# A transformer encoder block in fp32: where the last query and key turns of a head pair stand, which banks the turns use, and which engine squares the tokens

## The chip, the cores and the metric

The kernel runs on one core of a Trainium2 chip. The metric is the device time of one execution in microseconds. TensorE is PE in the profile, VectorE DVE, ScalarE ACT, GpSimd POOL, and SP issues most of the DMAs.

## What is computed

One encoder layer over 1024 tokens of width 1024. Half of the mixing width is neighbourhood attention with 8 heads of 64 on a token grid, the other half a multi-scale mean pooling; then an output projection and a gated feed-forward layer.

```python
for l in range(DEPTH):
    h = rms_norm(x, norm1_g[l])
    proj = h @ w_in[l]                       # q, k, v, u
    q = rms_norm(q, q_norm_g[l])             # per head
    k = rms_norm(k, k_norm_g[l])
    a = neighbourhood_attention(q, k, v, rpb[l])
    p = multiscale_pool(u, w_pool[l], pool_scale[l])
    x = x + jnp.concatenate([a, p], axis=-1) @ w_out[l]
    h2 = rms_norm(x, norm2_g[l])
    x = x + (jax.nn.silu(h2 @ w_gate[l]) * (h2 @ w_up[l])) @ w_down[l]
```

## The kernel before

Every fp32 product is made of three passes on operands that are split into a high part (a rounded cast, on ScalarE as a rule) and a low part (source minus high part, on VectorE): high by high, high by low, low by high (`mm3`, `split`). The names end in h and l: `xh`, `xl` for the tokens, `w1h`, `w1l` for projection weights, `kh`, `kl`, `qh`, `ql`, `vnh`, `vnl` for keys, queries and values, `wuh`, `wul` for the weights of u.

**Head.** Token chunks `xh[k]`, `xl[k]` (8 of them) and the weights of pair 0 are loaded, cast and split. The 8 token tiles of pair 0 stand in 8 PSUM banks (`pj_0_0` to `pj_0_7`); the first six are accumulated together, chunk by chunk, and the last two behind them. Meanwhile each token tile `xt` is squared and summed into `ssx`, from which `rstd` comes by `rsqrt` (lines 96 to 101). `pair(tt)` takes two tiles: squares of queries and keys and their sums, the values (`proj_vals`, L283 and L285), the norms (`proj_norm`, L270). `turn(tt)` (`proj_evac_b`) transposes the normalized queries and keys of two tiles on TensorE into a bank `qkt` (L91) and splits them into `qh`, `ql` (L311, L313) and `kh`, `kl` (L112, L113). Then `u_pool` projects u (bank `pu`), scales it, and pools it.

**Pairs 1 to 3.** `g_proj(p)` is a generator that yields after each three matmuls. It projects tile by tile (`pj_p_t`, 24 matmuls of 384 columns), the first two tiles `together`, and evacuates each with `finish`: a copy `qn` (L260), values, squares, norms, and behind each second tile the turn of the two tiles before. The last turn of a pair, that of tiles 6 and 7, is left in `late`. For the last pair tiles 5, 6 and 7 are projected together, with casts of output weights `wo` and of mixed inputs `mx` in between (`first_wo`).

**Attention** runs beside it, in 16 steps (4 pairs by 4 column blocks). `step(v)` writes scores of block v into four banks `s`, the values of block v - 2 into `po`, and the transposed probabilities of block v - 1 into three banks `pt`; between these parts `more(u)` draws units from the generators by the tables `FIRST`, `CYC` and, once the projections are done, `WCYC`, which draws the output products `pw`. `flush()` runs the turn in `late`: it is called ahead of each step with v % 4 == 3, and once more within `together`.

**Banks.** PSUM has three pools: `mmp` (3 banks: `pj`, `pu`, most `pw`), `stp` (4: scores, probabilities, and turns), `pop` (1: values). Work that takes a bank waits until the last readers of the tile that had it before are done.

**Order.** While `pin` is set, TensorE's instructions stay in program order, and likewise ScalarE's and VectorE's under `pin_act` and `pin_dve`; the others are placed by the compiler's scheduler. Each engine runs its own list in order. SP's DMAs wait for the tile that they write to be free and for the lane of an earlier DMA.

## Time and profile before

| what | us |
|---|---|
| three runs | 1038.33, 1038.53, 1041.15 (median 1038.53) |
| profiled execution | 1039.33 |
| its span | 1037.5 |
| TensorE busy | 1011.6 |
| VectorE busy | 656.4 |
| ScalarE busy | 416.3 |
| GpSimd busy | 392.4 |

The span runs from the first to the last instruction on the chip; about 1.8 us of the execution lie around it. In a timeline each row has the start, the duration, engine, line, operation, output and inputs, and in brackets how long the engine had been idle before and what ended that. The duration of a matmul is longer than the distance to the next one, as matmuls are pipelined; costs of matmuls are taken from distances. Rows with windows give the length of the window, the busy time (and number of instructions) of each engine, the TensorE clock that was granted (1.00 is full), the share of the DMA engines, and GB/s.

### The profile page before, as it was taken

What the parts mean: (1) busy time and instruction counts of PE and PEld (TensorE: products, weight loads), DVE (VectorE), ACT (ScalarE), POOL (GpSimd) and SP (SyncE); (2) the same over time, 40 slices, a digit from 0 to 9 for tenths busy, and PEclk for the clock granted to TensorE, in tenths of its full rate; (3) what the DMA queues carried; (4) which work ended last, traced back from release to release, by engine and by line L of the source; (5) the groups of instructions that cost most, each with busy time, mean ns of one, the idle gap of its engine ahead of it and who ended that gap; (6) DMA issues with size and microseconds to landing.
All of it is one profiled execution on the core that took longest, in us unless ns stands there. A gap on an engine that the chain in (4) does not pass through costs nothing.

```text
span 1037.5 us, 13512 instructions
## 1 busy us (share of the span) xinstructions
PE 1011.6 (98%) x4905; PEld 861.6 (83%) x4905; DVE 656.4 (63%) x1083; ACT 416.3 (40%) x820; POOL 392.4 (38%) x428
## 2 busy tenths in 40 slices
PE   9899989999799999999999999999999999999998
PEld 9788889899688887888888888888888888888887
DVE  5577766545754568866655545555462499978872
ACT  6532656545663235523332332332331254533400
POOL 0000433232361026466667568459545310000170
PEclk9999989989899999999999999999999999999999
DMA  9411633243721223113233133133126984373302
GB/s 359 164 36 41 198 86 93 61 143 132 254 72 61 107 108 115 57 62 125 98 115 137 63 120 134 71 122 112 72 81 198 340 274 155 118 244 110 134 31 91
DMA packets 52994, 132.22 MB, mean 127 GB/s; under 512 B 5632, under 2 KB 14592, under 8 KB 52928
## 3 DMA queue, kind: packets, MB, share of 16 engines
q1 hardware_dynamic: 46000, 106.97, 30.9%
q0 software_dynamic: 5632, 20.19, 5.3%
q10 hardware_dynamic: 1296, 4.20, 1.0%
q8 instruction: 38, 0.62, 0.2%
q14 instruction: 28, 0.23, 0.1%
HBM read 96.48 MB, written 30.67 MB: 123 GB/s over the span
## 4 chain that ended last, share of the span: by engine, by line
PE 91%; DMA 3%; DVE 3%; ACT 2%; issue 1%; SPq 1%; ACTq 0%; DVEq 0%
PE x L86 12%; PE w L86 12%; PE z L86 12%; PE pw L86 8%; PE pj L86 8%; PE y L86 6%; PE pc L86 6%; PE pa L86 6%; PE pd L86 6%; PE pu L86 4%; PE po L86 3%; PE pb L86 3%; PE s L86 2%; PE pt L91 1%; DMA raw_w<-in_w 1%; DMA raw_xt<-in_xt 1%
## 5 line engine op out<-in xcount | busy, mean ns | idle before, releaser
L86 PE MATMUL x<-b_h,w 128*128 128x512 f32 x352 | 115.6, 391 | 0.0
L86 PE MATMUL pw<-wo,mx 128*128 128x512 f32 x384 | 91.4, 393 | 0.2 <-ACT mx L725 0.2
L86 PE MATMUL pj<-w1h,xh 128*128 128x384 f32 x256 | 87.7, 347 | 0.0
L86 PE MATMUL pj<-w1l,xh 128*128 128x384 f32 x256 | 85.1, 337 | 0.0
L86 PE MATMUL pj<-w1h,xl 128*128 128x384 f32 x256 | 84.0, 337 | 0.0
L86 PEld LDWEIGHTS pw<-wo,mx 128*128 128x128 f32 x384 | 70.9, 188 | 14.8 <-ACT mx L725 0.6
L592 POOL TENSOR_SCALAR e<-e,r 64x128 f32<-64x128 f32 (+2 forms) x96 | 51.8, 555 | 80.6 <-DVE r L587 63.2
L1305 POOL TENSOR_TENSOR x2r<-x2r,u 128x512 f32<-128x512 f32 x12 | 23.8, 2025 | 149.8 <-DVE u L1263 149.8
L86 PEld LDWEIGHTS x<-b_h,w 128*128 128x128 f32 x352 | 65.9, 188 | 13.7
L86 PE MATMUL x<-b_l,w 128*128 128x512 f32 x176 | 68.7, 390 | 0.0
L1024 POOL TENSOR_TENSOR ur<-ur,gr 128x512 f32<-128x512 f32 x33 | 52.6, 1595 | 40.7 <-issue 22.0
L113 DVE TENSOR_TENSOR w_s<-sa,w_s 128x512 fp32r<-128x512 f32 x44 | 48.1, 1093 | 29.4 <-ACT w_s L112 29.2
L112 ACT CAST a_h<-raw_a 128x1024 fp32r<-128x1024 f32 (+1 forms) x42 | 41.0, 978 | 49.3 <-PE pc L86 13.8
L86 PE MATMUL z<-bt_h,w_s 128*128 128x512 f32 x176 | 57.8, 389 | 0.0
L86 PE MATMUL w<-bt_h,w_s 128*128 128x512 f32 x176 | 57.8, 389 | 0.0
L86 PE MATMUL y<-bt_h,w_s 128*128 128x512 f32 x176 | 57.8, 389 | 0.0
L86 PE MATMUL w<-b_h,w_s 128*128 128x512 f32 x176 | 57.8, 389 | 0.0
L86 PE MATMUL z<-bt_h,w 128*128 128x512 f32 x176 | 57.8, 389 | 0.0
L113 DVE TENSOR_TENSOR a_l<-raw_a,a_h 128x1024 fp32r<-128x1024 f32 (+1 forms) x42 | 49.7, 1188 | 3.4 <-DMA raw_d<-in_wd 2.9
L86 PEld LDWEIGHTS pj<-w1h,xh 128*128 128x128 f32 x256 | 48.8, 191 | 0.7 <-issue 0.5
L86 PEld LDWEIGHTS pj<-w1l,xh 128*128 128x128 f32 x256 | 48.4, 189 | 0.0
L86 PEld LDWEIGHTS pj<-w1h,xl 128*128 128x128 f32 x256 | 48.3, 189 | 0.0
(257 smaller groups left out, 2680.8 us busy)
## 6 DMA issues: line engine op xcount, KB each, us to landing
raw_a<-gsd SPq DMA_DIRECT2D x77, 256.0 KB, 3.6
raw_g<-in_wgu SPq DMA_DIRECT2D x22, 512.0 KB, 3.8
raw_u<-in_wgu SPq DMA_DIRECT2D x22, 512.0 KB, 4.0
gsd<-gr POOLq DMA_DIRECT2D x22, 512.0 KB, 4.0
raw_d<-in_wd SPq DMA_DIRECT2D x20, 512.0 KB, 4.1
nb<-in_rpbx SPq DMA_DIRECT2D x24, 384.0 KB, 3.7
raw_w<-in_w SPq DMA_DIRECT2D x15, 384.0 KB, 4.1
gsd<-ur POOLq DMA_DIRECT2D x11, 512.0 KB, 3.3
```

The lines of the kernel that those rows point to most:

```text
L86: i = nc.tensor.matmul(*a, **k)
L91: i = nc.tensor.transpose(*a)
L112: keep(nc.scalar.copy(h, src))
L113: keepd(nc.vector.tensor_tensor(out=l, in0=src, in1=h.bitcast(F32), op=ALU.subtract))
L592: nc.gpsimd.tensor_scalar(out=out, in0=in0, scalar1=s1, scalar2=1.0, op0=ALU.mult, op1=ALU.mult)
L1024: eng.tensor_tensor(out=res[i][c][:, l], in0=src, in1=g, op=ALU.mult)
L1305: nc.gpsimd.tensor_tensor(out=q, in0=q, in1=U2[c], op=ALU.add)
```

## The change

- The last turn of a pair moves within the step: it was ahead of the scores of v = 3, 7, 11 and is now between the other units and the probabilities of that step. It keeps a bank of `stp`; the three other turns of a pair take a bank of `mmp`.
- The squares of token tiles 1, 3, 5 and 7 are made by VectorE (a multiply with a sum along the row, new L491), those of 0, 2, 4 and 6 by ScalarE as before.
- In the head both last tiles of pair 0 are projected right behind the first six; statistics are split into `stats_a`, `stats_b` and `stats_c`, and the first chain of norms stands ahead of the casts of `wu` and `wp`. Turns 1 to 3 and the fourth `pair` are called from `u_pool`.
- For the last pair tiles 6 and 7 are projected together, and tile 5 by itself. `WCYC` has other numbers.

```diff
--- before.py
+++ after.py
@@ -31,13 +31,12 @@
 RQ = [[0, 1], [0, 1, 2], [1, 2, 3], [2, 3]]
 KE = 2
 W0 = 42
-KSS = 6
 WARM = 17
 CYC = [3, 3, 3, 4, 4, 4, 4, 4, 4, 4, 4, 5, 5, 5, 4, 4]
 R0 = 22
 FIRST = [3, 3, 4, 4, 4, 4, 4, 4, 4, 4, 4]
 CYC3 = CYC
-WCYC = [1] + [2] * 10 + [3]
+WCYC = [1, 4, 4, 1, 1] + [2] * 6 + [3]
 POOL_W = [2, 4, 8, 16]
 DGROUPS = [3, 4, 4]
 NPF = NFC // 2
@@ -224,20 +223,26 @@
 
     y8s = {}
 
-    def proj_stats(p, tt, pss, mid=None):
-        v8 = tq.tile([P, 8], F32, name=f"v8_{p}_{tt}", tag="v8")
-        y8 = tq.tile([P, 8], F32, name=f"y8_{p}_{tt}", tag="y8")
-        y8s[p, tt] = y8
-        for i, ps in enumerate(pss):
+    v8s = {}
+
+    def stats_a(p, tt, srcs):
+        v8s[p, tt] = []
+        for i, src in enumerate(srcs):
             t = 2 * tt + i
             sq = tq.tile([P, 256], F32, name=f"sq_{p}_{t}", tag="sq", bufs=2)
-            keep(nc.scalar.activation(sq, ps[:, :256], AF.Square))
+            keep(nc.scalar.activation(sq, src[:, :256], AF.Square))
             s4 = tq.tile([P, 4], F32, name=f"s4_{p}_{t}", tag="s4")
             keepd(
                 nc.vector.tensor_reduce(
                     out=s4, in_=sq.rearrange("p (h d) -> p h d", d=HD), axis=AX.X, op=ALU.add
                 )
             )
+            v8s[p, tt].append(s4)
+
+    def stats_b(p, tt):
+        v8 = tq.tile([P, 8], F32, name=f"v8_{p}_{tt}", tag="v8")
+        for i, s4 in enumerate(v8s[p, tt]):
+            t = 2 * tt + i
             keepd(
                 nc.vector.tensor_scalar(
                     out=v8[:, 4 * i : 4 * i + 4],
@@ -248,9 +253,12 @@
                     op1=ALU.add,
                 )
             )
-        if mid:
-            mid(p, 2 * tt, pss)
-        rsqrt(tq, y8, v8, 8, f"q{p}_{tt}")
+        v8s[p, tt] = v8
+
+    def stats_c(p, tt):
+        y8 = tq.tile([P, 8], F32, name=f"y8_{p}_{tt}", tag="y8")
+        y8s[p, tt] = y8
+        rsqrt(tq, y8, v8s.pop((p, tt)), 8, f"q{p}_{tt}")
 
     def new_qn(p, t):
         return tq.tile([P, 256], F32, name=f"qn_{p}_{t}", tag="qn", bufs=5)
@@ -293,10 +301,12 @@
             )
 
     def proj_evac_a(p, tt, pss):
-        proj_stats(p, tt, pss)
+        stats_a(p, tt, pss)
+        stats_b(p, tt)
+        stats_c(p, tt)
         proj_norm(p, tt, pss)
 
-    def proj_evac_b(p, tt, pool=stp):
+    def proj_evac_b(p, tt, pool=mmp):
         (kh, kl), (qh, ql) = kT[p], qT[p]
         qk = qks.pop((p, tt))
         pt = bank(pool, f"qkt_{p}_{tt}")
@@ -370,8 +380,8 @@
                 for i in range(2):
                     R = 2 * half + i
                     nc.vector.tensor_tensor(out=uv[:, R], in0=pv[:, i], in1=rv[:, R], op=ALU.mult)
-                if g == half == 0:
-                    hook()
+                if 2 * g + half < 3:
+                    hook(2 * g + half + 1)
 
         def u_win(g):
             u = us[g]
@@ -476,11 +486,16 @@
     ssx = cp.tile([P, NT], F32, name="ssx")
     for t in range(NT):
         raw = raws.pop(("xt", t))
-        keep(nc.scalar.activation(raw, raw, AF.Square, accum_out=ssx[:, t : t + 1]))
+        acc = ssx[:, t : t + 1]
+        if t % 2:
+            nc.vector.tensor_tensor_reduce(
+                out=raw, in0=raw, in1=raw, scale=1.0, scalar=0.0, op0=ALU.mult, op1=ALU.add, accum_out=acc
+            )
+        else:
+            keep(nc.scalar.activation(raw, raw, AF.Square, accum_out=acc))
     pin_act = False
     fetch_wu(1)
     proj_alloc(0)
-    cook_wu(0)
     pj = [bank(pl, f"pj_0_{t}") for t, pl in enumerate((mmp, mmp, mmp, stp, stp, pop, stp, stp))]
     pin = True
     for k in range(KC):
@@ -489,42 +504,47 @@
             for t in ts:
                 for i in h:
                     proj_pass(0, t, pj[t], k, i)
-        if k == KSS:
-            nc.vector.tensor_scalar(
-                out=vx, in0=ssx, scalar1=1.0 / DM, scalar2=EPS, op0=ALU.mult, op1=ALU.add
-            )
-            nc.vector.tensor_scalar(out=evx, in0=vx, scalar1=EPS, scalar2=None, op0=ALU.mult)
-            rsqrt(tq, rstd, vx, NT, "x")
-            nc.vector.scalar_tensor_tensor(
-                out=qscale, in0=gqk[:, 0:1], scalar=-(HD**-0.5), in1=gqk[:, 1:2], op0=ALU.mult, op1=ALU.mult
-            )
+    for t in (6, 7):
+        for k in range(KE, KC):
+            proj_mm(0, t, pj[t], k)
     pin_act = pin_dve = True
+    stats_a(0, 0, pj[:2])
+    keepd(nc.vector.tensor_scalar(out=vx, in0=ssx, scalar1=1.0 / DM, scalar2=EPS, op0=ALU.mult, op1=ALU.add))
+    keepd(nc.vector.tensor_scalar(out=evx, in0=vx, scalar1=EPS, scalar2=None, op0=ALU.mult))
+    stats_b(0, 0)
+    rsqrt(tq, rstd, vx, NT, "x")
+    stats_c(0, 0)
+    proj_norm(0, 0, pj[:2])
+    cook_wu(0)
+    keepd(
+        nc.vector.scalar_tensor_tensor(
+            out=qscale, in0=gqk[:, 0:1], scalar=-(HD**-0.5), in1=gqk[:, 1:2], op0=ALU.mult, op1=ALU.mult
+        )
+    )
+    proj_vals(0, 0, pj[:2])
 
     def pair(tt):
         pss = pj[2 * tt : 2 * tt + 2]
-        proj_stats(0, tt, pss, proj_vals)
+        stats_a(0, tt, pss)
+        stats_b(0, tt)
+        proj_vals(0, 2 * tt, pss)
+        stats_c(0, tt)
         proj_norm(0, tt, pss)
 
-    def turn(tt):
-        proj_evac_b(0, tt, (mmp, mmp, pop, stp)[tt])
-
-    pair(0)
+    proj_evac_b(0, 0)
     pair(1)
-    for k in range(KE, KC):
-        proj_mm(0, 6, pj[6], k)
-    turn(0)
     pair(2)
-    for k in range(KE, KC):
-        if k == 5:
-            turn(1)
-        proj_mm(0, 7, pj[7], k)
-    turn(2)
-    pair(3)
     pin = pin_act = pin_dve = False
     wp_hl = slot(F32R, "wp_hl", [P, 2, 4, P])
     wps += [wp_hl[:, 0], wp_hl[:, 1]]
     cook(("wp",), *wps)
-    u_win = u_pool(up, lambda: turn(3))
+
+    def hook(tt):
+        proj_evac_b(0, tt)
+        if tt == 1:
+            pair(3)
+
+    u_win = u_pool(up, hook)
 
     def attn_alloc(p):
         mf = slot(F32, f"mixf_{p}")
@@ -644,6 +664,8 @@
             values(*blocks[v - 2])
         more(4 * v)
         more(4 * v + 1)
+        if v % 4 == 3:
+            flush()
         if 0 < v <= len(blocks):
             transposes(*blocks[v - 1])
         more(4 * v + 2)
@@ -653,7 +675,7 @@
 
     def flush():
         while late:
-            proj_evac_b(late.pop(), 3)
+            proj_evac_b(late.pop(), 3, stp)
 
     def g_proj(p):
         proj_alloc(p)
@@ -679,7 +701,7 @@
                 finish(t, ps)
 
         yield from together((0, 1), lambda kk: flush() if kk == 2 else None)
-        for t in range(2, NT - 3 * last):
+        for t in range(2, NT - 2 * last):
             ps = bank(mmp, f"pj_{p}_{t}")
             for k in range(KC):
                 proj_mm(p, t, ps, k)
@@ -696,7 +718,7 @@
                 if t == 6:
                     cook_w1(p + 1, 0)
         if last:
-            yield from together((5, 6, 7), first_wo)
+            yield from together((6, 7), first_wo)
         late.append(p)
         if p + 1 < NPAIR:
             for i in range(1, 4):
@@ -860,8 +882,6 @@
             run(WCYC[min(u - W0 - 1, len(WCYC) - 1)])
 
     for v in range(len(blocks) + 1):
-        if v % 4 == 3:
-            flush()
         step(v, more)
     run(1000)
     values(*blocks[-1])
```

VectorE, head. In the kernel before these rows follow each other (`xl_197`, `xl_205` and `xl_209` are chunks 5, 6 and 7; `w1l_3` the weights of the last two chunks):

```order
L173 SCALAR_TENSOR_TENSOR xl_193<-raw_x_130,sm_sb,xh_192 128x1024
L173 SCALAR_TENSOR_TENSOR xl_197<-raw_x_132,sm_sb,xh_196 128x1024
L113 TENSOR_TENSOR w1l_3_201<-raw_w_0_3_134,w1h_3_200 128x768
L173 SCALAR_TENSOR_TENSOR xl_205<-raw_x_136,sm_sb,xh_204 128x1024
L173 SCALAR_TENSOR_TENSOR xl_209<-raw_x_138,sm_sb,xh_208 128x1024
```

In the changed kernel, from the same row on (`raw_xt_142` and `raw_xt_146` are token tiles 1 and 3, and L491 is the square, with its sum in a second row):

```order
L172 SCALAR_TENSOR_TENSOR xl_193<-raw_x_130,sm_sb,xh_192 128x1024
L491 ISA raw_xt_142,ssx<-raw_xt_142 128x1024
L491 ISA ssx 128x1
L172 SCALAR_TENSOR_TENSOR xl_197<-raw_x_132,sm_sb,xh_196 128x1024
L112 TENSOR_TENSOR w1l_3_201<-raw_w_0_3_134,w1h_3_200 128x768
L491 ISA raw_xt_146,ssx<-raw_xt_146 128x1024
L491 ISA ssx 128x1
L172 SCALAR_TENSOR_TENSOR xl_205<-raw_x_136,sm_sb,xh_204 128x1024
L172 SCALAR_TENSOR_TENSOR xl_209<-raw_x_138,sm_sb,xh_208 128x1024
```

Two squares now stand among the splits: that of tile 1 ahead of chunk 5, that of tile 3 ahead of chunk 6.

TensorE, step 3, as pair 2 is projected beside pair 0's attention. Before, the scores follow the turn (`qkt_3_1634` is the last turn of pair 1, of whose four transposes the last two are shown; `s_3` are the scores of pair 0's block 3; the three rows ahead of the turn are those of the next piece):

```order
L91 MATMUL qkt_3_1634<-ident,qn_6_1508 128x128
L91 MATMUL qkt_3_1634<-ident,qn_7_1560 128x128
L86 MATMUL s_3_0_0_1643<-kh_225,qh_223 128x384
L86 MATMUL s_3_0_1_1644<-kh_225,qh_223 128x384
L86 MATMUL s_3_0_0_1643<-kl_226,qh_223 128x384
L86 MATMUL s_3_0_1_1644<-kl_226,qh_223 128x384
```

In the changed kernel the projection rows are followed at once by the scores:

```order
L85 MATMUL pj_1_1624<-w1h_0_1512,xh_162 128x384
L85 MATMUL pj_1_1624<-w1l_0_1513,xh_162 128x384
L85 MATMUL pj_1_1624<-w1h_0_1512,xl_163 128x384
L85 MATMUL s_3_0_0_1634<-kh_225,qh_223 128x384
L85 MATMUL s_3_0_1_1635<-kh_225,qh_223 128x384
L85 MATMUL s_3_0_0_1634<-kl_226,qh_223 128x384
```

and the turn (`qkt_3_1717`, its last two transposes) comes later in the step, behind 18 more projections and right ahead of the probabilities `pt_2`:

```order
L90 MATMUL qkt_3_1717<-ident,qn_6_1508 128x128
L90 MATMUL qkt_3_1717<-ident,qn_7_1560 128x128
L90 MATMUL pt_2_0_1726<-ident,e_2_0_0_1449 128x128 x3
L90 MATMUL pt_2_0_1726<-ident,e_2_1_0_1462 128x128
L90 MATMUL pt_2_2_1728<-ident,e_2_1_0_1462 128x128
L90 MATMUL pt_2_1_1727<-ident,e_2_0_1_1453 128x128 x3
```

The scores, the values and 18 projections have passed ahead of the turn.

VectorE, last pair. Before, the norms of tiles 4 to 7, `kl` of turn 2 and `ql` of turn 3 stand in this order, ahead of the score reductions (L574) of block 3:

```order
L270 TENSOR_TENSOR qn_4_2795<-qn_4_2795,y_3_2_3024 128x256
L270 TENSOR_TENSOR qn_5_3019<-qn_5_3019,y_3_2_3024 128x256
L99 TENSOR_TENSOR rsq_q_3_3072<-y_3_3_3061 128x8
L100 SCALAR_TENSOR_TENSOR rsq_q_3_3072<-rsq_q_3_3072,v_3_3_3060 128x8
L101 SCALAR_TENSOR_TENSOR y_3_3_3061<-rsq_q_3_3072,y_3_3_3061 128x8
L270 TENSOR_TENSOR qn_6_3052<-qn_6_3052,y_3_3_3061 128x256
L270 TENSOR_TENSOR qn_7_3056<-qn_7_3056,y_3_3_3061 128x256
L313 SCALAR_TENSOR_TENSOR ql_2338<-qkt_2_3080,qscale,qh_2337 128x4x64
L113 TENSOR_TENSOR wo_1_1_3455<-raw_wo_1_3177,wo_1_0_3454 128x512 x2
L113 TENSOR_TENSOR kl_2340<-qkt_2_3080,kh_2339 128x256
L313 SCALAR_TENSOR_TENSOR ql_2338<-qkt_3_3103,qscale,qh_2337 128x4x64
L574 ISA e_3_0_0_3130,m_3_0_0_3131<-s_3_0_0_3112,nb_3_0_2908 128x384
```

In the changed kernel `kl` of turn 2 (the last row) stands behind the score reductions of block 3 (L594, pair 2):

```order
L594 ISA e_3_1_0_3134,m_3_1_0_3135<-s_3_1_0_3105,nb_3_1_2934 128x384
L594 ISA m_3_1_0_3135 128x1
L594 ISA e_3_1_1_3138,m_3_1_1_3139<-s_3_1_1_3106,nb_3_1_2934 128x384
L594 ISA m_3_1_1_3139 128x1
L323 SCALAR_TENSOR_TENSOR ql_2338<-qkt_2_3080,qscale,qh_2337 128x4x64
L750 TENSOR_TENSOR mx_0_1_3029<-mixf_1798,mx_0_0_3028 128x512
L750 TENSOR_TENSOR mx_0_1_3029<-mixf_1136,mx_0_0_3028 128x512
L247 TENSOR_SCALAR v_3_3_3068<-s_3_7_3066,evx 128x4
L607 RECIPROCAL r_3_0_3120<-sm_3_0_3119 128x2
L112 TENSOR_TENSOR wo_0_1_3047<-raw_wo_0_2989,wo_0_0_3046 128x512 x2
L607 RECIPROCAL r_3_1_3133<-sm_3_1_3132 128x2
L112 TENSOR_TENSOR kl_2340<-qkt_2_3080,kh_2339 128x256
```

Turn 2's queries and keys are now split behind reductions, splits of mixed inputs and of output weights; turn 3 comes later still.

## The prediction

> **What bounds the kernel now.** I read the page first, then TensorE's row in the view of waits.
>
> ```profile
> PE 1011.6 (98%) x4905; PEld 861.6 (83%) x4905; DVE 656.4 (63%) x1083; ACT 416.3 (40%) x820; POOL 392.4 (38%) x428
> ```
> ```profile
> PE qkt L91 <- DVE qn L270: 10.3, 3, 5.4
> PE qkt L91 <- ACT vnh L283: 3.1, 1, 3.1
> PE s L86 <- DVE kl L113: 2.6, 3, 1.4
> PE s L86 <- DVE m L574: 1.8, 3, 0.7
> ```
>
> TensorE is busy 98% of the span and no other engine over 63%, so the end moves only where TensorE stops waiting or runs faster. The change touches four groups of waits: columns are the total, the number and the longest, 17.8 us together. The windows then show what a wait costs behind itself (second-last but two columns: granted clock).
>
> ```profile
> 40.30:43.80 3.50, 3.50 (x12) 2.86 (x11) 2.95 (x11) 1.79 (x7) 0.00 (x0) 0.51 0.02 5
> ```
> ```profile
> 149.00:153.00 4.00, 4.00 (x15) 3.56 (x16) 1.89 (x9) 2.55 (x8) 1.25 (x3) 0.50 0.50 139
> ```
> ```profile
> 210.00:214.00 4.00, 4.00 (x16) 3.61 (x14) 1.34 (x6) 2.15 (x9) 1.28 (x4) 0.50 0.62 171
> ```
> ```profile
> 266.00:270.00 4.00, 2.36 (x10) 1.38 (x10) 3.55 (x15) 1.91 (x6) 0.00 (x0) 0.50 1.04 333
> ```
>
> Behind each wait for `qkt` the clock is halved, for about 3.5 us or more. Behind the 1.38 us wait for `kl`, at 119.91, it stays whole:
>
> ```profile
> 119.90:123.30 3.40, 3.39 (x20) 3.16 (x21) 3.40 (x13) 2.65 (x8) 1.03 (x2) 1.00 0.45 126
> ```
>
> So a wait of 2.4 to 5.4 us is paid twice, once idle and once slow.
>
> **Last turn of pairs 1 and 2.** Here TensorE's timeline shows the whole stage.
>
> ```profile
> 141.55 0.42 PE L86 MATMUL pj<-w1h,xh 128*128 128x384 f32 x1
> ...
> 145.73 1.10 PE L91 MATMUL qkt<-ident,qn 128*128 128x128 f32 x4 [2.35 <-DVE qn L270]
> ...
> 148.85 0.69 PE L86 MATMUL s<-kh,qh 64*128 64x384 f32 x1 [0.45 <-DVE m L574]
> ...
> 153.27 0.34 PE L86 MATMUL pj<-w1h,xh 128*128 128x384 f32 x1
> ...
> 156.40 0.82 PE L91 MATMUL pt<-ident,e 128*128 128x128 f32 x6
> ```
> ```profile
> 250.55 0.44 PE L86 MATMUL s<-kh,qh 64*128 64x384 f32 x2
> ...
> 251.80 0.38 PE L86 MATMUL po<-pt_h,vnh 128*128 128x256 f32 x1
> ...
> 253.66 0.34 PE L86 MATMUL pj<-w1h,xh 128*128 128x384 f32 x1
> ```
> ```profile
> 201.55 0.60 PE L91 MATMUL qkt<-ident,qn 128*128 128x128 f32 x4
> 201.90 0.42 PE L86 MATMUL pj<-w1h,xh 128*128 128x384 f32 x1
> ```
>
> From 141.55 to the probabilities at 156.40 go 14.85 us. The work in it at full clock: 27 projection matmuls (9 ahead, 18 behind; the last 18 take 156.40 - 153.27 = 3.13, so 0.174 each, 4.69 in all), four transposes 0.35 (201.55 to 201.90), one score block 1.25 and one value block 1.86 (from 250.55 on): 8.15 us. So 6.7 us are idle or slow. The change puts the same pieces in the order: 9 projections, scores, values, 18 projections, turn, probabilities. The turn is then asked for 4.69 + 3.11 = 7.8 us after 141.55, at 149.35 or later.
>
> ```profile
> 142.70 0.35 DVE L285 SCALAR_TENSOR_TENSOR vnl<-pj,rstd,vnh 128x128 fp32r<-128x128 f32 x1
> ...
> 145.16 0.76 DVE L270 TENSOR_TENSOR qn<-qn,y 128x256 f32<-128x256 f32 x2
> ```
>
> Its `qn` was ready at 145.92; the score reductions now come ahead of it on VectorE, four at 0.48 (below), so about 147.9: 1.5 us early, no wait. New is a wait of projections: two mmp banks are left for tiles while `qkt` holds the third, so pair 2's tile 1 needs `vnl` of pair 1's tile 7, done at 143.05, and TensorE is there after 6 matmuls, at 142.59: 0.46. The moved turn issues four transposes, two copies on ScalarE, two subtractions on VectorE and no DMA; the next score block, its reader, comes a whole step later than it. Saved: 6.7 - 0.5 = **6.2 us**.
>
> ```profile
> 206.27 0.85 PE L91 MATMUL qkt<-ident,qn 128*128 128x128 f32 x4 [2.56 <-DVE qn L270]
> ...
> 217.21 1.04 PE L91 MATMUL pt<-ident,e 128*128 128x128 f32 x8
> ```
> ```profile
> 203.25 0.35 DVE L285 SCALAR_TENSOR_TENSOR vnl<-pj,rstd,vnh 128x128 fp32r<-128x128 f32 x1
> ```
>
> Pair 2 is the same code: 217.21 - 201.90 = 15.31 less 8.15 is 7.2; the new wait ends at 203.60, TensorE comes at 202.94: 0.7. Saved: **6.5 us**. With `qkt` off the score banks, three short waits go too, each of a score block for a bank held by a turn or by the block before: the 1.4 for `kl` near 119.9, and two of 0.7 for `m`; nothing is late in their place that I could find: **2.7 us**.
>
> **The last pair.** TensorE idles 5.42 us for `qn`, then does turns, scores and values at half clock.
>
> ```profile
> 261.56 0.60 PE L91 MATMUL qkt<-ident,qn 128*128 128x128 f32 x4
> 267.57 2.49 PE L91 MATMUL qkt<-ident,qn 128*128 128x128 f32 x8 [5.42 <-DVE qn L270]
> ...
> 276.50 2.92 PE L86 MATMUL pw<-wo,mx 128*128 128x512 f32 x12
> ```
>
> From 261.91 (0.35 behind 261.56) to 276.50 are 14.6 us, for work of 0.70 + 1.25 + 1.86 = 3.8: 10.8 lost. Tiles 6 and 7 together, not 5, 6 and 7, bring the norms forward: turn 2 runs without a wait. But VectorE's work is crowded into a shorter stage, and the third tile of the output product takes turn 2's bank, so it waits for `kl` of turn 2, which stands in VectorE's order behind four score reductions, casts and splits.
>
> ```profile
> L113 DVE TENSOR_TENSOR wo<-raw_wo,wo 128x512 fp32r<-128x512 f32 x12 | 9.2, 802 | 3.4 <-ACT wo L112 3.1 <-PE s L86 0.3
> ```
> ```profile
> 253.45 0.55 DVE L574 CUSTOM_DVE_ANT_0 e<-s,nb 128x384 f32<-128x384 f32 x1
> ...
> 253.93 0.69 DVE L728 TENSOR_TENSOR mx<-yr,mx 128x512 fp32r<-128x512 f32 x1
> 254.53 0.55 DVE L574 CUSTOM_DVE_ANT_0 e<-s,nb 128x384 f32<-128x384 f32 x1
> ```
>
> Tile 6's last matmul is at about 260.7 in old times, and its `vnl` some 1.1 us later (a copy, a cast and a subtraction). From there to that `kl` VectorE has seven splits of 128x512 at 0.60 (253.93 to 254.53), four reductions at 0.48 (253.45 to 253.93) and some 2.2 us of small ones: 8.3, so `kl` at 270.1.
>
> ```profile
> 244.13 1.25 PE L91 MATMUL pt<-ident,e 128*128 128x128 f32 x10
> ...
> 245.14 0.42 PE L86 MATMUL pj<-w1h,xh 128*128 128x384 f32 x1
> ```
>
> TensorE does two blocks of probabilities (1.01 each, 244.13 to 245.14), 69 projections, two turns, two blocks of scores and of values and six products (twelve span 2.92, the row at 276.50) from 244.13 on: 2.0 + 12.0 + 0.7 + 2.5 + 3.7 + 1.4 = 22.3, so it asks at 266.5. I put the new wait at 3.5 us; from 0, if VectorE keeps ahead, to 5.4, the wait removed. At over 2.35 us it should halve the clock once, 1.7. Saved: 10.8 - 3.5 - 1.7 = **5.6 us**.
>
> **The head.** Removed: the wait of the first turn, and half a clock window behind it (the row 40.30:43.80), 3.06 + 1.7 = 4.8 us, as both last tiles are now projected ahead of it. The price is on VectorE.
>
> ```profile
> 23.77 0.33 PE L86 MATMUL pj<-w1h,xl 128*128 128x384 f32 x1
> ```
> ```profile
> 21.57 0.33 SPq L120 DMA_DIRECT2D raw_wu<-in_wu  x1
> 22.84 0.33 SPq L120 DMA_DIRECT2D raw_wp<-in_wpool  x1
> ```
> ```profile
> L173 DVE SCALAR_TENSOR_TENSOR xl<-raw_x,sm_sb,xh 128x1024 fp32r<-128x1024 f32 x7 | 9.0, 1285 | 2.0 <-ACT xh L172 1.7
> L113 DVE TENSOR_TENSOR wul<-raw_wu,wuh 128x1024 fp32r<-128x1024 f32 x3 | 3.7, 1221 | 1.2 <-ACT wuh L112 1.2
> ```
>
> In the new order the square of token tile 1 stands ahead of `xl` of chunk 5. That tile lands at 22.84 (`raw_wp` is issued when its DMA's lane comes free); a multiply and sum of 128x1024 isn't in the trace, so I take the 1.22 of the split of that size; bounds are 0.55 (the score reduction, three eighths of the size) and 2.5 (twice the split). Then `xl` ends at 22.84 + 1.22 + 1.29 = 25.35, and TensorE wants it at 23.77: 1.6 us new, 0.9 to 2.9, and 0.25 at the next chunk. The casts of `wu` and `wp`, moved behind the first norms, cost nothing as long as the two tiles projected first (36 matmuls, 6.3 us) cover them; without the cover it is the split's 1.22. Near 54 us the turns, splits and products on `rstd` queue up on VectorE, and turn 2 and the third bank of `pu` wait for them, about 2.3 us together. 4.8 - 1.6 - 0.25 - 2.3 = +0.65; one halved window would make it -1.0. I take **0**; from -5 to +2.
>
> The trace has idle gaps of 1.38 that leave the clock whole and of 2.35 that halve it; the new ones lie between or little over. [...]
>
> The new table for the output products issues as many matmuls as before, six of them earlier; I cost it at nothing, since the probabilities between them are waited for only if ScalarE falls behind (rival 1).
>
> **Sum.** 6.2 + 6.5 + 2.7 + 5.6 + 0 = 21 us. The profiled execution took 1039.33, its span 1037.5 and 1.8 around it: 1018.3. That execution lies 0.8 over the median shown (1038.53), so the same sum for the median is 1017.5; as not all may come, I say **1018.5**.
>
> **The rivals.**
> 1. The new wait in the last pair is larger: the `wo` loads and ScalarE's casts are late too (the DMA row 266:270 has a share of 1.04), the wait is 5.4 and the clock halves for three windows: that stage saves nothing, 1024. Chance 0.13.
> 2. The head's squares are slow (2.5 us each) and the clock drops twice: 1018.5 + 5 = 1023.5. For: VectorE is in order and now waits for a DMA. Chance 0.10.
> 3. The new waits don't halve the clock: head +1, last pair +1.7, and the last pair's wait is 2: 1014. Chance 0.10.
> 4. The change doesn't do what it says: `qn` of the last turn isn't ready at its new place, since VectorE does the score block first. Margin 1.5 us; over that the wait and slow clock return in pairs 1 and 2: 1018.5 + 12.7 = 1031. Chance 0.04.
> 5. Slower: each tile of pairs 1 to 3 now waits for the evacuation two tiles back, as `qkt` has one of three banks. A tile takes 24 x 0.174 = 4.2 us; a wait arises where evacuation takes longer, and from 0.95 us in each of 22 tiles on it is slower than before; at 1.1 each 1042.7. Against: `vnl` at 143.05 came 1.85 us behind its tile's last matmul (141.55 - 0.35). Chance 0.03.
>
> The forecast (1015 to 1022) keeps 0.60. The range 1012 to 1027 takes in cases 1 to 3; it leaves out 4, 5 and some of each tail. About 0.3%, 3.1 us, can be told from no change: faster 0.93, same 0.04 (part of 4 and 5), slower 0.03.
>
> **What would show it.** The waits of `qkt` for `qn` are gone from pairs 1 and 2, and the windows after them show a clock of 1.00; `pj` waits for `vnl` there, under 1 us. In the last pair `pw` waits for `kl`, 3 to 4 us. In the head `pj` waits for `xl` near 23.8, about 1.6. It is wrong if TensorE's waits sum to more than 14 us, or if a wait of `pj` recurs in every tile.

## The result and the profile after

| kernel | median, us | runs | ratio to before, 95% interval |
|---|---|---|---|
| before | 1038.43 (1038.33 to 1041.15) | 4 | |
| after | 1022.12 (1021.18 to 1024.05) | 4 | 0.9839 (0.9817 to 0.9861) |

The change is 1.6% faster. The time is 3.6 us over the forecast of 1018.5, 0.1 over the band of 1015 to 1022 that held most of the chance, and inside the range of 1012 to 1027. The profiled execution of the changed kernel took 1024.05, the slowest of its four; its span is 1022.3, against 1037.5 before: 15.2 us less.

First the page's line of the engines after the change:

```profile
PE 1001.6 (98%) x4905; PEld 853.9 (84%) x4905; DVE 663.5 (65%) x1091; ACT 411.3 (40%) x812; POOL 392.7 (38%) x428
```

Then TensorE's waits in the changed kernel: what waited, for what, the total in us, how often, and the longest.

```profile
PE s L85 <- DVE pt_l L112: 4.7, 3, 4.2
PE pw L85 <- DVE rsq_q L98: 4.5, 1, 4.5
...
PE pu L85 <- DVE kl L112: 1.4, 1, 1.4
...
PE pj L85 <- ACT xh L171: 1.1, 1, 1.1
...
PE pj L85 <- DVE xl L172: 0.5, 1, 0.5
PE pj L85 <- DVE vnl L293: 0.4, 1, 0.4
```

The reader sees that all three waits of `qkt` for `qn` are gone, with the short ones of `s` for `kl` and `m`. Two large ones stand in their place: the foreseen one of the output product (it is put down to `rsq_q`, which ended with it; `kl` of turn 2 is the instruction just before), and one of 4.2 us of scores for `pt_l`, which the prediction did not have. The sign of being wrong that the prediction named first, waits that sum to more than 14 us, did show: all rows of this view sum to 16.8, 4.7 of them for `pt_l`. The other one, a wait of `pj` in every tile, did not.

The windows of the changed kernel at the last turns of pairs 1 and 2, behind the two large waits, and at the place near the end where the clock was halved before (409 to 412.5 us then). The third number from the right is the granted clock.

```profile
141.00:145.00 4.00, 4.00 (x32) 3.74 (x29) 3.60 (x16) 3.10 (x12) 1.23 (x3) 1.00 0.28 72
193.50:197.50 4.00, 4.00 (x31) 3.50 (x30) 3.66 (x17) 2.86 (x10) 0.57 (x3) 1.00 0.20 22
253.90:257.40 3.50, 3.49 (x9) 2.77 (x10) 1.79 (x4) 0.00 (x0) 2.55 (x6) 0.54 1.00 365
278.50:282.00 3.50, 3.48 (x13) 3.02 (x14) 3.31 (x11) 1.59 (x5) 0.00 (x0) 0.50 0.38 142
282.00:285.50 3.50, 3.50 (x14) 3.10 (x13) 1.54 (x4) 2.10 (x7) 0.44 (x1) 0.66 0.00 0
396.50:400.00 3.50, 3.41 (x27) 2.79 (x26) 3.21 (x6) 3.33 (x7) 3.50 (x3) 1.00 0.19 75
```

In pairs 1 and 2 the clock is now whole. In the last pair it is halved once at the wait of `pw` and twice at the wait for `pt_l`.

The loss by the clock comes in equal pieces. Adding one minus the clock over windows of 1 us gives 1.71 us, or two or three times that, at each place where the clock fell, in every run: a stretch of 3.41 us at half speed (one more begins within 1 us of the end of each span; it is left out). So each trace can be written as TensorE's idle time, plus 1.71 for each such stretch, plus a rest that changes by a few us at most. All runs of the whole kernel, with the sums that I made from their traces (idle: gaps over 0.03 us; the last column is span less idle less 1.71 a stretch; spans and sums are those of the one profiled execution, which can lie a few us from the median):

| run | median, us | ratio (95%) | span | idle | half-clock stretches | rest |
|---|---|---|---|---|---|---|
| before | 1038.43 | | 1037.5 | 22.0 | 9 | 1000.1 |
| after | 1022.12 | 0.9839 (0.9817 to 0.9861) | 1022.3 | 17.1 | 3 | 1000.1 |
| e1 old table | 1018.34 | 0.9803 (0.9789 to 0.9818) | 1017.2 | 11.8 | 2 | 1002.0 |
| e2 splits on VectorE | 1019.27 | 0.9816 (0.9801 to 0.9830) | 1019.3 | 14.0 | 2 | 1001.9 |
| e3 squares on ScalarE | 1020.36 | 0.9823 (0.9799 to 0.9848) | 1019.2 | 15.3 | 2 | 1000.5 |
| e4 turn alone | 1028.01 | 0.9900 (0.9885 to 0.9914) | 1025.8 | 17.4 | 5 | 999.9 |
| e5 turns in score banks | 1026.58 | 0.9884 (0.9867 to 0.9901) | 1024.8 | 16.0 | 3 | 1003.7 |
| e6 three tiles, old table | 1023.91 | 0.9853 (0.9835 to 0.9871) | 1019.1 | 14.6 | 3 | 999.4 |
| e7 splits behind, old table | 1020.95 | 0.9825 (0.9802 to 0.9847) | 1020.2 | 13.6 | 3 | 1001.5 |
| e8 and third tile later | 1021.85 | 0.9829 (0.9815 to 0.9842) | 1019.5 | 13.4 | 3 | 1001.0 |
| e9 norms on ScalarE | 1023.38 | 0.9846 (0.9821 to 0.9872) | 1022.2 | 15.1 | 4 | 1000.3 |
| e11 e8 with e9 | 1018.35 | 0.9793 (0.9771 to 0.9815) | 1016.3 | 11.6 | 2 | 1001.3 |

Of the change's 15.2 us, 4.9 are idle time and six stretches are 10.3: two thirds of the gain is clock. The rest moves by up to 4.3 us from run to run, most in e5; what moves it is not shown, so differences of 2 to 4 us between two runs are read from their waits and stretches too, not from the times alone.

### The profile page after: what moved, and what is told of

The parts are those of the page before. It is cut to its first block, busy times and chain, and to the rows that moved or that the text cites. A ratio compares the mean times of both kernels' runs of the same rounds, so it can differ in the third digit from the quotient of the medians.

```text
span 1022.3 us, 13490 instructions
## 1 busy us (share of the span) xinstructions
PE 1001.6 (98%) x4905; PEld 853.9 (84%) x4905; DVE 663.5 (65%) x1091; ACT 411.3 (40%) x812; POOL 392.7 (38%) x428
## 4 chain that ended last, share of the span: by engine, by line
PE 92%; DMA 4%; DVE 1%; ACT 1%; issue 1%; SPq 0%; POOL 0%; DVEq 0%; POOLq 0%; ACTq 0%
PE x L85 12%; PE w L85 12%; PE z L85 12%; PE pj L85 11%; PE pw L85 7%; PE y L85 6%; PE pc L85 6%; PE pa L85 6%; PE pd L85 6%; PE pu L85 4%; PE pb L85 3%; PE po L85 3%; PE s L85 2%; PE pt L90 1%; DMA raw_xt<-in_xt 1%; DMA vsh<-vnh 1%
## 5 line engine op out<-in xcount | busy, mean ns | idle before, releaser
L85 PE MATMUL pw<-wo,mx 128*128 128x512 f32 x384 | 93.6, 399 | 4.7 <-DVE rsq_q L98 4.5
L85 PEld LDWEIGHTS x<-b_h,w 128*128 128x128 f32 x352 | 65.9, 188 | 13.4
```

The costliest lines, as they stand in the source:

```text
L85: i = nc.tensor.matmul(*a, **k)
```

## Where the time went, by stage

TensorE's timeline of the changed kernel gives the starts of the third, fifth, seventh, ninth and eleventh block of scores, and of the first transposes behind the attention:

```profile
127.77 0.45 PE L85 MATMUL s<-kh,qh 64*128 64x384 f32 x2
...
152.69 0.44 PE L85 MATMUL s<-kh,qh 64*128 64x384 f32 x2
...
179.99 0.45 PE L85 MATMUL s<-kh,qh 64*128 64x384 f32 x2
...
205.87 0.44 PE L85 MATMUL s<-kh,qh 64*128 64x384 f32 x2
...
233.13 0.44 PE L85 MATMUL s<-kh,qh 64*128 64x384 f32 x2
...
380.12 0.38 PE L90 MATMUL ht_t<-ident,t 128*128 128x128 f32 x2
```

In the kernel before, the same places (the eleventh block, at 250.55, is shown in the prediction):

```profile
130.68 0.45 PE L86 MATMUL s<-kh,qh 64*128 64x384 f32 x2
...
161.77 0.44 PE L86 MATMUL s<-kh,qh 64*128 64x384 f32 x2
...
190.17 0.44 PE L86 MATMUL s<-kh,qh 64*128 64x384 f32 x2
...
222.59 0.44 PE L86 MATMUL s<-kh,qh 64*128 64x384 f32 x2
...
393.74 0.38 PE L91 MATMUL ht_t<-ident,t 128*128 128x128 f32 x2
```

So the two-block stretch with pair 1's last turn fell from 31.09 to 24.92 us, that with pair 2's from 32.42 to 25.88: 6.2 and 6.5, as predicted to the tenth. At the start of the eleventh block the changed kernel is 17.4 us ahead; 1.1 of that was there at 69 us, the head's. From there to the transposes it falls back to 13.6: the last pair, which should have given 5.6, takes 3.8. Behind it one more stretch of half clock is missing (the row 396.50:400.00), 1.7.

What happens in the last pair is read from VectorE's and GpSimd's timelines of the changed kernel, ahead of the 4.2 us wait:

```profile
273.95 3.23 DVE L750 TENSOR_TENSOR mx<-yr,mx 128x512 fp32r<-128x512 f32 x1 [0.58 <-POOL mx L750]
277.10 0.68 DVE L802 TENSOR_TENSOR x<-pw,x 128x512 f32<-128x512 f32 x1
277.70 1.00 DVE L112 TENSOR_TENSOR pt_l<-pt,pt_h 128x512 fp32r<-128x512 f32 x2
```
```profile
273.89 0.71 POOL L612 TENSOR_SCALAR e<-e,r 64x128 f32<-64x128 f32 x2
274.58 0.82 POOL L564 TENSOR_SCALAR nb<-nb 128x768 f32<-128x768 f32 x1
275.37 1.25 POOL L750 TENSOR_TENSOR mx<-yr,mx 128x512 fp32r<-128x512 f32 x1
```

VectorE has a low part of the mixed inputs and an addition in front of the two `pt_l` that free the score banks. The split, which takes 0.69 us elsewhere, takes 3.23: it ends 0.56 us behind the last of four GpSimd instructions that run beside it. From its start to the second `pt_l` VectorE does not pause, so 2.5 of the 4.2 us are what this split takes over its usual 0.69. So two causes are at hand: the order, which puts this split ahead of `pt_l`, and GpSimd beside it.

## The experiments

Each edit is against the changed kernel, but for e4, which is against the one before.

**e1: the old table of output products.**

```diff
-WCYC = [1, 4, 4, 1, 1] + [2] * 6 + [3]
+WCYC = [1] + [2] * 10 + [3]
```

> The changed kernel with the old WCYC. Theory A: the unforeseen wait of scores for pt_l (4.20 us at 278.52) comes from the new table: it brings forward the end of the first output products, so that a split of mx and an addition stand ahead of pt_l on VectorE. With the old table pt_l stands first: the wait is under 0.5 us, the halved clock behind it is gone, the time falls by 4 to 7 us to 1015 to 1018. Rival B: GpSimd's work beside VectorE's split is what delays pt_l, whatever the table: a wait of 2 us or more stays there and the time is 1020 or more. The wait of pw behind kl (4.5 us at 253.9) stays under both.

Measured 1018.34, against 1022.12: 3.8 us faster than the change as made, a little less than the 4 to 7 expected. Each run of e1 is below each run of the change, though the two intervals of the ratio just touch. TensorE's waits in that run:

```profile
PE pw L85 <- DVE rsq_q L98: 4.7, 1, 4.7
...
PE pj L85 <- DVE vnl L293: 0.7, 2, 0.4
PE pj L85 <- DVE xl L172: 0.5, 1, 0.5
```

The wait for `pt_l` is gone from the list (one of 0.13 is left, too small for it), and the wait for `pw` is where it was. With the new table the first two calls of `more` in step 11 draw four units of products each in place of two, and with them more of VectorE's work comes ahead of the probabilities. It is a loss by itself. Theory A had `pt_l` first in VectorE's order, and that is not so: a split of `mx` still stands ahead of it, but it takes 0.68 us, and no addition stands between:

```profile
272.09 0.68 DVE L750 TENSOR_TENSOR mx<-yr,mx 128x512 fp32r<-128x512 f32 x1
272.69 1.60 DVE L112 TENSOR_TENSOR pt_l<-pt,pt_h 128x512 fp32r<-128x512 f32 x3
```

So e1 shows that the table brings the wait about; whether by the order or by the long split it doesn't tell.

**e2: low parts of the mixes' second halves all on VectorE**, none on GpSimd, with the new table kept.

```diff
-                    split_mix(six[2 * t + i // 3], 1, nc.scalar, (nc.gpsimd, nc.vector)[i // 3])
+                    split_mix(six[2 * t + i // 3], 1, nc.scalar, nc.vector)
```

> The changed kernel with all low parts of the second half of the mixed inputs made by VectorE, none by GpSimd; table unchanged. Rival B (contention with GpSimd): the split that took 3.23 us takes 0.7, the wait of scores for pt_l at 278.5 falls under 1.5 us, time 1015 to 1018. Theory A (order): the splits are still ahead of pt_l on VectorE, now more of them; the wait stays at 2 us or more, time 1020 or more.

Measured 1019.27, between the two ranges. The waits for `pt_l` sum to 1.4 in three pieces, the longest 0.8, and no half-clock stretch stands behind them. Four splits of `mx` stand ahead of `pt_l` here, and none is long:

```profile
271.17 1.43 DVE L750 TENSOR_TENSOR mx<-yr,mx 128x512 fp32r<-128x512 f32 x2 [0.28 <-PE pt L90]
272.99 1.47 DVE L750 TENSOR_TENSOR mx<-yr,mx 128x512 fp32r<-128x512 f32 x2 [0.39 <-ACT mx L747]
```

That is rival B's picture. A half-clock stretch near 391 us, which the change doesn't have, is 1.7 us of this run's time. But the compiler's scheduler also put VectorE's instructions in another order, so this alone doesn't separate the two causes.

**e3: all token squares on ScalarE**, as before the change.

```diff
-        if t % 2:
+        if False:
```

> The changed kernel with all eight token squares on ScalarE again. My theory: VectorE's squares cost the 0.5 us wait of pj for xl and gain ScalarE four squares of 1.28 us; without them the wait for xl is gone, the first norms come up to 1.5 us later but the two last tiles cover that, so the time stays within 1.5 us of 1022. Rival: ScalarE's squares are what held the first norms, the first turn waits 1 to 3 us again and the clock halves: 1024 to 1027.

Measured 1020.36, 1.6 under 1022 where at most 1.5 was expected; its interval overlaps that of the change, and the rival is out. At the start of pair 0's pooling (`py`) the profiled run is 1.1 us earlier than the change: 0.5 is the wait for `xl`, which is gone, and 0.2 a shorter wait for `xh`. VectorE's squares show no gain, and in the head a loss of about 1 us. The order further on changed too: there the wait for `pt_l` is 2.3 us, and it comes at 265 us, one block earlier.

**e4: only the last turn moved, in the kernel before.**

```diff
+        if v % 4 == 3:
+            flush()
         if 0 < v <= len(blocks):
             transposes(*blocks[v - 1])
...
-        if v % 4 == 3:
-            flush()
         step(v, more)
```

> The kernel before with nothing but the last turn moved beside the probabilities. My theory: the two waits of qkt for qn of 2.4 and 2.6 us and the halved clock behind them go, 12 to 13 us: 1025 to 1027; the 5.4 us wait of the last pair stays. Rival: without banks of their own the turns of tiles 0 to 5 still sit in the score banks, the move alone makes the scores wait for kl instead, and under half of that comes: 1032 or more.

Measured 1028.01, 10.9 us (1.0%) under its own runs of the kernel before (1038.93): about two thirds of the whole gain comes from this one move. It is 1 us above the range of the theory and far from the rival's. TensorE's waits for `qn` are left only in the head (2.1) and in the last pair (5.3); the short ones for score banks stay, and that for `kl`, near 120 us, is longer than before (1.9 in place of 1.4) and now has a half-clock stretch behind it, 1.7 us:

```profile
PE qkt L91 <- DVE qn L270: 7.4, 2, 5.3
PE s L86 <- DVE m L574: 2.3, 3, 0.9
PE s L86 <- DVE kl L113: 1.9, 1, 1.9
```

**e5: the turns of pairs 1 to 3 in the score banks again.**

```diff
-    def proj_evac_b(p, tt, pool=mmp):
+    def proj_evac_b(p, tt, pool=None):
+        pool = pool or (stp if p else mmp)
```

> The changed kernel, with the turns of pairs 1 to 3 in the score banks again, as before; where the turns stand in the order of work is not altered. Theory A (the move out of the score banks is worth what the short waits were): the waits of score blocks for kl and for m come back, 1.4 + 2 x 0.7 = 2.8 us, and the two short waits of projections for vnl (0.4) and the wait of the output product for kl of turn 2 (4.5) change, as its third tile gets another bank: with the product's wait gone too, the two nearly cancel, and the time is between 1020 and 1025. Theory B (only the place of the turn counts, the bank is nothing): the time is that of the changed kernel less the product's wait, 1017 to 1019.

Measured 1026.58. Both theories forecast less. The wait of `pw` is gone as expected, but the short waits return larger than before: the one for `kl` has 2.0 us and a half-clock stretch behind it, and in the last pair scores wait for `m` (2.2 of the 3.5) and for `pt_l`:

```profile
PE s L85 <- DVE m L595: 3.5, 3, 2.2
PE s L85 <- DVE pt_l L112: 2.5, 4, 1.1
PE s L85 <- DVE kl L112: 2.0, 1, 2.0
```

So by the medians the move to other banks is worth 4.5 us in all (1026.58 less 1022.12). That it is worth what the short waits were is not shown: by the table e5 has 1.1 us less idle time than the change and as many half-clock stretches, and a rest 3.6 us greater, of which the cause stays open.

**e6: tiles 5, 6 and 7 together again, with the old table.**

```diff
-        for t in range(2, NT - 2 * last):
+        for t in range(2, NT - 3 * last):
...
-            yield from together((6, 7), first_wo)
+            yield from together((5, 6, 7), first_wo)
```

> The changed kernel with the old table for the output products, and with tiles 5, 6 and 7 of the last pair computed together again. To be compared with the old table alone (1018.3). Theory A (the norms of turn 2 come too late when three tiles end together): the wait of qkt for qn in the last pair comes back, about 5 us, with half a clock window behind it, while the wait of the output product for kl (4.7 us) goes, since it is the same VectorE work that is late: 1018 to 1023, and the chain shows qn in place of kl. Theory B (the two groupings are equal for VectorE's total work, so nothing is won by the new one): within 1 us of 1018.3. A time over 1020 speaks for A.

Measured 1023.91, against 1018.34 of e1 (ratios 0.9853 and 0.9803, intervals apart); the two profiled executions are 2.4 us apart, that of e6 being the fastest of its five. The wait of `qkt` for `qn` returns with 4.3 us and that of `pw` goes; two half-clock stretches stand there in place of one. This is theory A's picture, at a time 0.9 over its range. The new grouping is a gain, but it changes one wait on VectorE for another.

**e7: splits behind kl**, with the old table.

```diff
-            first_mix((0, 1))
-        if kk == 3:
-            cook_wo(0, 0)
...
                 yield
+                if i == 3 and g is gs[0]:
+                    first_mix((0, 1))
+                if i == 3 and g is gs[1]:
+                    cook_wo(0, 0)
```

> The changed kernel with the old table, and in the last pair the first splits of the mixes and of wo are issued behind the first three matmuls of the output product, not ahead of turn 2: then kl of turn 2 stands ahead of them in VectorE's order. Theory A (pw waits because these splits stand ahead of kl): its wait falls from 4.7 to about 2 us and the clock behind it stays higher; 1014 to 1017 against 1018.3 for the old table alone. Theory B (VectorE's total work up to the probabilities sets the stage, in whatever order): the wait moves on to pt_l or mx, and the time is 1018 or more.

**e8: as e7, and the third tile's first product behind four of the others'.** The splits are issued two units of products earlier than in e7.

```diff
-        for i in range(len(six)):
-            for g in gs:
-                next(g)
-                yield
+        for n, j in enumerate((0, 1, 0, 1, 2, 2, 0, 1, 2, 0, 1, 2, 0, 1, 2, 0, 1, 2)):
+            next(gs[j])
+            yield
+            if n == 7:
+                first_mix((0, 1))
+            if n == 8:
+                cook_wo(0, 0)
```

> As the run before, and the third tile of the output product, which takes the bank of turn 2, has its first matmul behind four of the other two tiles' instead of behind two. Theory A: TensorE comes later to the bank, its wait for kl falls under 1.5 us, no clock window is halved in that stage, and the time is 1012 to 1016. Theory B (VectorE is late with everything in that stage): a wait of the same length arises elsewhere in the last pair, and the time is within 1 us of the run before.

Measured 1020.95 and 1021.85: the times of theory B for both, and theory A's are out. In e7 the wait of `pw` fell to 2.7, in e8 it is gone (turn 2 waits 3.2 for `qn` there); but TensorE then waits 3.2 and 2.3 us for `pt_l`, with another half-clock stretch. VectorE's timeline of e8 shows the pair of splits in front:

```profile
267.37 5.55 DVE L112 TENSOR_TENSOR wo<-raw_wo,wo 128x512 fp32r<-128x512 f32 x2 [0.34 <-ACT wo L111]
272.85 1.28 DVE L112 TENSOR_TENSOR pt_l<-pt,pt_h 128x512 fp32r<-128x512 f32 x2
```

and GpSimd's beside it:

```profile
266.15 2.77 POOL L612 TENSOR_SCALAR e<-e,r 128x384 f32<-128x384 f32 x6 [7.76 <-DVE r L607]
268.89 1.64 POOL L564 TENSOR_SCALAR nb<-nb 128x768 f32<-128x768 f32 x2
270.49 1.28 POOL L750 TENSOR_TENSOR mx<-yr,mx 128x512 fp32r<-128x512 f32 x1
```

Two splits of 0.69 take 5.55 us; the first has 4.95 of it and ends 0.55 us behind GpSimd's last instruction, as in the changed kernel. In e7 the same split takes 4.93. So it need not be VectorE's total work, as theory B has it, that makes the wait. This asked for experiments on GpSimd.

**e9: the last pair's norms on ScalarE**, new table kept.

```diff
+                    if p == 3:
+                        return nc.scalar.activation(out, in0, AF.Copy, scale=s1)
                     nc.gpsimd.tensor_scalar(
```

> The changed kernel (new table), with the normalisations of the probabilities of the last pair (line 612) on ScalarE, not on GpSimd; VectorE keeps its order up to the stage in question, and there the split of mx (line 750) still stands ahead of the last two pt_l. Theory A (that split, 3.23 us instead of 0.69, is held up by the run of GpSimd instructions beside it): with fewer of them it takes at most 2.1 us (0.82 and 1.25 of GpSimd may still stand ahead), TensorE's wait for pt_l falls from 4.2 to under 2 us, and the time is 1017.5 to 1020.5. Theory B (the order on VectorE alone makes the wait): the wait stays at 3.5 us or more, and the time is within 1.5 us of the changed kernel's 1022.1. Theory C (ScalarE becomes late with pt_h): TensorE waits for pt_h or po, time over 1022.

Measured 1023.38. Theory A was right on the instruction and wrong on the time. The split took 0.68 us:

```profile
276.52 0.68 DVE L750 TENSOR_TENSOR mx<-yr,mx 128x512 fp32r<-128x512 f32 x1
```

and the wait for `pt_l` fell to 2.0. But ScalarE's casts for the probabilities came later, the additions of `pw` were now ahead of the split, and the remaining 0.34 and 1.62 us of idle time still cost two half-clock stretches; a second one stands behind `pw`. ScalarE's row shows the last two casts, of which the first ended only at 276.49, against 274.16 in the change:

```profile
275.92 0.84 ACT L111 CAST pt_h<-pt 128x512 fp32r<-128x512 f32 x2
```

So theory C has a part in it. What VectorE's order alone would cost with this table is not shown by e9; in e2, with the splits ahead and none of them long, it was 1.4 us and no clock.

**e11: e8 with e9.** The old table, the later third tile, and the last pair's norms on ScalarE.

> The run with the third tile's first product later (1021.9, on a chip where the kernel before took 1039.6), with the normalisations of the last pair on ScalarE as well. There one split of wo took 4.95 us beside GpSimd's work, and TensorE waited 2.3 us for pt_l behind it. Theory A (GpSimd's run holds it up): that split takes under 2.2 us, the wait for pt_l goes or is under 0.7, the clock stays at 1.00 there, and the time falls by 2 to 4.5 us, to a ratio of 0.979 to 0.981 against before. Theory B (the order alone): within 1 us of that run, ratio 0.982 to 0.984.

Measured 1018.35, ratio 0.9793, against 0.9829 of e8 (the intervals touch): theory A. VectorE's timeline has the same two splits with 1.92 us in place of 5.55,

```profile
267.76 1.92 DVE L112 TENSOR_TENSOR wo<-raw_wo,wo 128x512 fp32r<-128x512 f32 x2 [1.36 <-ACT wo L111]
```

the wait for `pt_l` is 0.7 (2.3 in e8), and the stretch of half clock behind it is gone. It is the lowest ratio of all runs, below the change and the kernel before; from e1 it can't be told apart.

**e10 and e12: the price of GpSimd beside VectorE, alone.** Small programs, with GpSimd multiplies queued and one VectorE subtraction of 128x512 released beside them; e10's expectation is the first below, e12's the second.

> Only a small program, none of the block: a 128x512 subtraction on VectorE that is released by a GpSimd instruction, with 0, 1, 2, 4 and 8 further GpSimd multiplies of 128x384 (about 0.65 us each) queued right behind the releasing one; once with both operands in SBUF, once with one of them in PSUM; all of it twice. Theory A (VectorE's instruction with two SBUF operands cannot start while GpSimd has work queued): about 0.69 us with none, then 0.69 plus 0.65 for each queued multiply, so about 3.3 with four and 5.9 with eight; the one with an operand in PSUM stays at 0.69 throughout. Theory B (it waits for one GpSimd instruction at most): never over 1.4 us. Theory C (the two share the bandwidth): both kinds grow slowly, to some 1.3 us, and GpSimd's own multiplies get longer.

> Again only a small program, none of the block. The first one released VectorE's subtraction at the end of a GpSimd instruction, and VectorE took 0.69 us each time while GpSimd's next multiply grew from 0.59 to 1.12. Here ScalarE releases it within a run of 3, 5 or 8 GpSimd multiplies of 128x384, or within 4 of 128x768; and once GpSimd's own subtraction does, with the same instructions behind it as in the changed kernel at 273.9 us (two multiplies of 64x128, one of 128x768, a subtraction of 128x512). All with both operands in SBUF, and with one in PSUM. Theory A (whichever engine holds the way to SBUF keeps it as long as it has work queued): released within the run, VectorE's subtraction ends only behind the run's last multiply: it takes some 1.5 us with 3, 2.7 with 5 and 4.4 with 8; with PSUM 0.69 always. Theory B (the way is granted anew with each instruction): 0.69 plus at most the rest of one multiply, so under 1.3 us in all of them, and GpSimd is held by 0.5 once; then the 3.23 and 4.9 us are something that these programs do not have, and stay open.

In e10, released at the end of a GpSimd instruction, VectorE took 0.69 us each time; here with four multiplies queued, which take 2.28 us when VectorE reads one operand from PSUM, and 2.81 here:

```profile
14.73 2.81 POOL L36 TENSOR_SCALAR g<-g,sc 128x384 f32<-128x384 f32 x4
```

In e12, released within a multiply of a run of eight:

```profile
16.11 1.08 DVE L42 TENSOR_TENSOR lo<-src,hi 128x512 fp32r<-128x512 f32 x1 [2.31 <-ACT hi L51]
```

With an operand in PSUM it was 0.69 in all fifteen. So the times are those of theory B of the last run: in these programs the delay did not grow with the number of multiplies queued. VectorE took 1.08 beside a run of five as beside one of eight, 0.4 over its 0.69, and in e10 GpSimd's run grew by 0.5 once, whether it had one multiply (1.12 against 0.59 with PSUM) or eight (5.05 against 4.52). The sequence of the changed kernel, rebuilt, gave 0.69 three times out of three. What makes VectorE wait for a whole run of GpSimd instructions is not shown by these programs.

## Why the prediction held, and where it failed

- **What bounds it: right.** Idle time of TensorE and the clock behind it account for the difference between before and after, whose rests are both 1000.1; over all rows of the table the rest stays between 999.4 and 1003.7 us, though idle time goes from 11.6 to 22 and the stretches from 2 to 9.
- **Pairs 1 and 2: right in mechanism and size**, 6.2 and 6.5 against 6.2 and 6.5. The new wait for `vnl` came in pair 2 with 0.43 (0.7 predicted) and not in pair 1. That the figures agree to the tenth is luck: in pair 1 the 6.7 us counted as lost were 6.2 by the idle time and two stretches (2.35, 0.45 and 3.41), and the wait of 0.5 taken off did not come. `qn` was ready at 144.5 and asked for at 146.9, with more room than the 1.5 us foreseen. Rival 4 is out.
- **Short waits: right, 0.9 us too small.** They are gone. By the starts of the blocks they gave 3.6 us (17.4 less 1.1, 6.2 and 6.5), where 2.7 was predicted; this figure is what is left over, so small errors of the others are in it.
- **Head: taken as 0, came out at +1.1.** The multiply and sum, guessed at 1.22 us from a split, took 1.23, and `xl` ended at 25.2 (25.35 predicted):

```profile
22.78 1.23 DVE L491 CUSTOM_DVE_ANT_0 raw_xt<-raw_xt 128x1024 f32<-128x1024 f32 x1 [5.94 <-DMA raw_xt<-in_xt]
23.93 1.28 DVE L172 SCALAR_TENSOR_TENSOR xl<-raw_x,sm_sb,xh 128x1024 fp32r<-128x1024 f32 x1
```

  TensorE waited 0.5 for it, not 1.6. It was itself 1.1 us late by a wait for `xh` of the second chunk, whose load varies (0 to 1.1 us over the runs); but in e1 and e11, without that wait, it waited only 0.5 and 1.0 as well. The waits for `u` and `kl`, 0.3 and 1.4, sum to 1.7, against 2.3. Rival 2 is out.
- **The new wait in the last pair: right in place, 1 us short in size.** Predicted: TensorE asks at 266.5 and `kl` comes at 270.1, in old times; less the 17.4 us that the stage is ahead, 249.1 and 252.7. VectorE's and TensorE's timelines of the changed kernel:

```profile
253.37 0.40 DVE L112 TENSOR_TENSOR kl<-qkt,kh 128x256 fp32r<-128x256 f32 x1
```
```profile
253.91 5.41 PE L85 MATMUL pw<-wo,mx 128*128 128x512 f32 x16 [4.54 <-DVE rsq_q L98]
```

  TensorE asked at 249.37 (253.91 less 4.54), `kl` ended at 253.77: 4.5 in place of 3.5, with the clock halved once, as said. The work in front took 9.15 us, from `vnl` of tile 6 (244.62) to the end of `kl`, where 8.3 was counted. Six of the seven splits took the 0.60 each that they were counted at; one split, and one small instruction that took 0.22 at 245.91, took longer beside GpSimd:

```profile
244.92 1.07 DVE L750 TENSOR_TENSOR mx<-yr,mx 128x512 fp32r<-128x512 f32 x1
...
251.34 0.79 DVE L247 TENSOR_SCALAR v<-s,evx 128x4 f32<-128x4 f32 x1
```

  Rival 1 named this wait, but with three halved stretches and late `wo` loads. One stretch came; a `wo` load did hold ScalarE until 257.95, but TensorE's wait was over by then.
- **The step that failed: "the new table for the output products ... I cost it at nothing, since the probabilities between them are waited for only if ScalarE falls behind".** They are waited for through VectorE: 4.2 us for `pt_l` and two half-clock stretches, 3.4, so 7.6. With the 1 us of the row above and two small waits of 0.5 this is the distance between the 5.6 promised and the 3.8 lost, 9.4, to within 0.3. With the old table alone, e1 goes from 15.8 us ahead at the eleventh block to 18.9 at the transposes: 3.1 gained where the change lost 3.8, so 6.9 of the 7.6 are the table's. TensorE's waits sum to 11.5 us there, under the bound of 14. (The medians differ by less, 3.8: the change's profiled execution is 1.9 over its median, and e1 lost a stretch of half clock in the head.) That GpSimd is a part of it is shown by e11 beside e8, by e2, and by the split itself in e9. Whether the order would cost a stretch without it is not shown: in e9 ScalarE is late as well, and in e2 none was lost there.
- **Not in the sum:** one half-clock stretch less near 396 us, 1.7 us, with the same two waits (1.0 and 1.5) in front as before; e2, e5, e6, e8 and e11 have that stretch, e1, e3, e4, e7 and e9 don't. It is luck, of the kind shown under the clock below.
- **Why the total was nearer than its terms.** The profiled execution gained 15.3 us of the 21 in the sum. The last pair's miss alone is 9.4; the head (1.1), the short waits (0.9) and the stretch near 396 us (1.7) came out better by 3.7. That leaves 5.7 in the profiled execution; the 1 us taken off the sum, and a profiled execution 1.9 over its median where 0.8 was reckoned with, leave 3.6.

## What to carry to other kernels

Price a new order on the engine that feeds the bound engine, not only on the bound engine: put VectorE's list of the stage beside TensorE's, and see which instruction that frees a bank now stands behind new work. Count a wait as its length plus whole stretches of half clock (1.71 us lost in each here), and look for the order that keeps the idle time within any 3.4 us small (in these traces, over 1.81 us in one of the pieces counted below was followed by half clock every time). Where one part of a change can be undone in one line, do it: here that line was worth as much as a quarter of the gain.
